# One run for each step of a merge, a decay mask by select, and a cast on ScalarE, in a hybrid DeltaNet and pooling block

## The chip, the cores and the metric

The kernel runs on one core of a Trainium2 chip. The metric is the device time of one execution in microseconds (us), the median of three runs. The engines are TensorE (PE in the rows, its weight loads PEld), VectorE (DVE), ScalarE (ACT), GpSimd (POOL), and SyncE (SP), which issues the DMAs.

## The reference

One layer over 1024 latent tokens of width 1024, with 256 context tokens ahead of them that use the same weights:

```
hn   = rms_norm(h, gain) * (1 + scale) + shift
proj = hn @ w_in                    # q, k, v | a, b | z_dn | u_pool | z_pool
q, k, v = split(silu(conv5(qkv)));  q, k = l2(q), l2(k)
o_f  = gated_delta_rule(q, k, v, g[0], beta[0], s_f)     # 8 heads of 128
o_b  = the same, backwards, from s_b                     # s_f, s_b: states after the context
o    = rms_norm(o_f + o_b, dn_gain) * silu(z_dn)
y_p  = (group-wise (box_mean(u_pool) - u_pool) @ pool_w) * pool_scale * silu(z_pool)
out  = rms_norm(x + gate * (concat(o, y_p) @ w_out), final_gain)

# gated_delta_rule, in chunks:
decay = exp(where(row >= col, g_row - g_col, -inf))
a     = where(row > col, (k*beta) @ k.T * decay, 0)
u, w  = solve(I + a, [v*beta, k*beta*exp(g)])
v_new = u - w @ S;   o = (q*exp(g)) @ S + (q @ k.T * decay) @ v_new
S     = S * exp(g_last) + (k*exp(g_last - g)).T @ v_new
```

## The kernel before

The products of the projections are fp32, made of three passes of a faster type: every operand is split into a high part, a copy in the type FP32R, and a low part, the difference, and high by high, low by high and high by low are summed. In the rows `hnhi, hnlo` are the parts of the normalised, transposed input, `wraw, whi, wlo` a weight tile and its parts (ScalarE makes `whi`, GpSimd `wlo`), and `mm` is the sum in PSUM. The input's own split stands in `x_half`, which transposes x by TensorE into `pp` and has ScalarE write the modulated input into `tmp`, `W`, `XT` or `Y`, and `x_split`, which copies that into `hnhi` and subtracts.

The delta rule works on chunks of 128 positions: 8 chunks of one head in both directions are one job, 8 heads and 2 context jobs make 10. For each job `stage_d` loads differences of summed decays into the tiles `D0` and `D1` (rows: `D`), masks them and takes the exponential. After a tile of k has been multiplied it is convolved on VectorE (`kT<-u,cw,kT`), goes through a tanh on ScalarE (`u<-kT`) and a last product (`kT<-u,kT`). Then `stage_a` multiplies k by itself (`pa<-kT`) and inverts the triangular matrices bottom up: blocks of 16 merge into blocks of 32 with products of 16 and 32 rows and columns (`pa<-laneN,B`, `pa<-laneN,bt`, `pa<-t,XT`), and `stage_b` merges 32 into 64 and 64 into 128 (`pp` from `W`, `B`, `Y`, `VV`). These are the small products: they use a corner of TensorE's array. A scan over the 8 chunks then carries the state (`sc<-S,kT`, `o<-S,qd`, `sc<-r,B`, `sc<-y,ks`, `o<-y,D`). A finished head is normalised (squares `junk<-o`, a power `sm<-sm,expo`, scaling `ks<-o,sm`), transposed (`pp<-ident,ks`) and multiplied by its gate (`zs<-pp,dng,zs`).

The order of each engine's instructions is fixed when the program is built. A planner (`Flow`) runs the generators of all these stages side by side: each `yield` is a place at which a thread may rest while another one issues, and a main thread supplies products of the projections in between. The planner keeps a modelled clock for each engine and charges every instruction with the price that `Engine.cost` returns; an instruction is put in when its inputs are ready by that clock. `yield REST` in `stage_a` and `stage_b` divides a step of a merge into groups of 16 or 8 small products, and the other work comes between. A helper records all operations, so every row of the profile has the same line, L364, and the rows are told apart by their tiles.

Of the kernel before, what the change touches and what calls it, by code (L numbers as in the profile page):

```python
# [27 lines left out]
TAKE = ("bank",)  # L28
RB = 8
REST = 340.0  # L30
NEXT = dict(pe=200.0, act=200.0, dve=200.0, pool=120.0)
# [282 lines left out]
class Engine:  # L314
    def __init__(self, flow, real, name):
        self.flow, self.real, self.name = flow, real, name

    def cost(self, op, a, k):
        out = k["out"] if "out" in k else a[0]
        n = _size(out)  # L320
        if self.name == "pe":
            if op == "transpose":
                return 108.0
            rhs = a[2] if len(a) > 2 else k["rhs"]
            n = _size(rhs)
            if rhs.dtype == FP32R:
                return max(107.0, 0.417 * n)
            m = int(out.shape[0])
            return max(1.67 * m, 1.67 * n) if m > 32 or n > 64 else max(0.83 * m, 0.83 * n)
        ptr = any(not isinstance(k.get(i), (float, int, type(None))) for i in ("scale", "bias", "scalar", "scalar1"))  # L330
# [12 lines left out]
        if op == "tensor_copy":  # L343
            return 80.0 + 3.8 * n
        if op == "memset":
            return 36.0 + 0.83 * n
# [44 lines left out]
def kernel(  # L391
# [90 lines left out]
    ident = const.tile([P, P], FP32, name="ident")  # L482
    mask = [const.tile([P, P], FP32, name=f"mask{d}") for d in range(2)]
    tri = [dl_tile([P, P], "S", 2) for d in range(2)]
# [48 lines left out]
    for d in range(2):  # L533
        pool.memset(mask[d], 0.0)
        pool.memset(tri[d], 1.0)
        s = 1 if d == 0 else -1
        pool.affine_select(out=mask[d], in_=mask[d], pattern=[[s, P]], compare_op=ALU.is_ge, fill=NEG,
                           base=0, channel_multiplier=-s)
        pool.affine_select(out=tri[d], in_=tri[d], pattern=[[s, P]], compare_op=ALU.is_ge, fill=0.0,
                           base=0, channel_multiplier=-s)  # L540
# [428 lines left out]
    def stage_d(J, part):  # L969


        t = J.PT[part] = dl_tile([P, 2, 4, P], f"D{part}", 2)
        r = J.h * (NB if J.is_x else NBC)
        for d in range(2):
            rd = r + 4 * (part ^ d)
            sync.dma_start(out=t[:, d].rearrange("p b i -> p (b i)"), in_=gscr[J.is_x][d, rd:rd + 4, :].rearrange(
                "b i -> (b i)").partition_broadcast(P))
        yield
        for d in range(2):
            pool.tensor_tensor(out=t[:, d], in0=t[:, d], in1=rep(mask[d], 4), op=ALU.add)  # L980
            if d or DY < 8:
                yield
            for b in range(4):
                act.activation(out=t[:, d, b, :], in_=t[:, d, b, :], func=ACTF.Exp,
                               bias=J.col("ngc", d, 4 * (part ^ d) + b))
                if b % DY == DY - 1:
                    yield "act" if XACT & 16 else None
        flow.flag("D", J.key, part)

    def stage_a(J):  # L990
# [103 lines left out]
        for d in range(2):  # L1094
            for b in range(8):
                for r in range(4):
                    w = tb[h16[r], b, :] if d else B[h16[r], 0, b, Q[r]]
                    pe.matmul(pv[Q[r], d, b, :], w, W16[h16[r], 8 * d + b, :], start=True, stop=True)
                if b % 4 == 3:
                    yield REST  # L1100
        yield
# [4 lines left out]
        for d in range(2):  # L1106
            for b in range(8):
                for r in range(4):
                    pe.matmul(pv2[Q[r], d, b, :], XT[Q[r], d, b, :], G[Q[r], d, b, :], start=True, stop=True)
                if b % 4 == 3:  # L1110
                    yield REST
        yield
# [17 lines left out]
    def stage_b(J):  # L1130
# [6 lines left out]
        for b in range(8):  # L1137
            for s in range(2):
                lo, hi = Q[2 * s], Q[2 * s + 1]
                pe.matmul(pv[hi, b, 0:32], B[lo, 0, b, hi], W[lo, 0, b, :], start=True, stop=True)  # L1140
                pe.matmul(pv[lo, b, 0:32], B[hi, 1, b, lo], WT[hi, b, :], start=True, stop=True)
            if b % 4 == 3:
                yield REST
        yield
# [5 lines left out]
        for b in range(8):  # L1150
            for s in range(2):
                lo, hi = Q[2 * s], Q[2 * s + 1]
                pe.matmul(pv[lo, b, 0:32], Y[hi, b, 0:32], B[hi, 0, b, hi], start=True, stop=True)
                pe.matmul(pv[hi, b, 0:32], Y[lo, b, 0:32], W[lo, 1, b, :], start=True, stop=True)
            if b % 4 == 3:
                yield REST
        yield TAKE
# [18 lines left out]
        for b in range(8):  # L1176
            pe.matmul(pv[h1, b, :], B[h0, 0, b, h1], VV[h0, b, :], start=True, stop=True)
            pe.matmul(pv[h0, b, :], B[h1, 1, b, h0], VV[h1, b, :], start=True, stop=True)
            if b % 4 == 3:
                yield REST  # L1180
        flow.flag("merged", J.key)
# [6 lines left out]
        for b in range(8):  # L1188
            pe.matmul(pv[h0, b, :], Y[h1, b, :], B[h1, 0, b, h1], start=True, stop=True)
            pe.matmul(pv[h1, b, :], Y[h0, b, :], B[h0, 1, b, h0], start=True, stop=True)  # L1190
            if b % 4 == 3:
                yield REST
        yield
# [194 lines left out]
    def x_half(hf):  # L1388
        for k in range(KT):
# [9 lines left out]
            if XACT & 4:  # L1399
# [3 lines left out]
                           scale=md[:, 0, 1, k:k + 1], bias=md[:, 0, 0, k:k + 1])  # L1403
            flow.give()
            flow.flag("h32", n)
            flow.add(x_split(hf, k, h32), [("h32", n)], True)

    def x_split(hf, k, h32):
        if XACT & 8:
            yield "dve"  # L1410
        dve.tensor_copy(hn[2 * hf][:, k, :], h32)
        yield
        e = dve if k % XD == 0 else pool
# [70 lines left out]
    def thread_a():  # L1484
# [3 lines left out]
        for k in range(-2, H):  # L1488
            yield ("k", k)
            yield ("ab", k >= 0)  # L1490
            yield ("done", k - 2)
            yield from stage_a(jobs[k])

# [589 lines left out]
```

## Time and profile before

| | |
|---|---|
| runs | 1317.15 us median, 1315.63 to 1318.1 |
| the profiled execution | 1321.76 us, span 1320.0 us |
| TensorE busy | 1212.5 us, 92% of the span |
| VectorE, ScalarE, GpSimd busy | 928.0, 570.8, 438.7 us |
| to 55 us | modulation of the inputs |
| 55 to 165 us | context, transposes and split of x |
| 165 to 1003 us | the eight heads |
| 1003 to 1146 us | pooling |
| 1146 to 1320 us | output projection |

A row of the timeline gives the start, the duration, engine, operation, tiles, the shape and how many alike stood together; in brackets the idle time ahead and what ended it. Matmuls overlap in the array, so what one costs is the distance between two starts (its pitch), not its duration. The rows count a small product or one of 128x128, which run in fp32, as two.

### The profile page before, as it was taken

The numbers are of one execution on the slowest core, as the hardware profiler recorded it, in microseconds if no ns is written. First come the engines' busy times: TensorE is split into PE (matmuls) and PEld (weight loads), VectorE is DVE, ScalarE is ACT, GpSimd is POOL, SyncE is SP. The second block draws the span as 40 slices with busy tenths as digits, with TensorE's granted clock in tenths as the row PEclk, the third lists the DMA queues.
The fourth block names the chain that finished last, engine by engine and source line by source line (L and its number), as shares of the span: only waits on it lengthen the run. The fifth ranks groups of instructions, "written<-read, shape, count | busy, mean of one in ns | idle before, by whom it ended". The sixth has DMA issues, their size and how long they took to land.

```text
span 1320.0 us, 26398 instructions
## 1 busy us (share of the span) xinstructions
PE 1212.5 (92%) x10631; PEld 977.8 (74%) x10631; DVE 928.0 (70%) x1883; ACT 570.8 (43%) x1498; POOL 438.7 (33%) x451
## 2 busy tenths in 40 slices
PE   8876699899899999999999989999999999799997
PEld 2666577677777877788778768778788777688887
DVE  4799989868886787877776867878433999724212
ACT  3466437444436547455474464643613123322110
POOL 2477433230421423314132233141215454402330
PEclk9788899899999999989999999999999899899999
DMA  9533344223121213212221131212313135565230
GB/s 329 188 99 93 86 140 125 74 57 90 37 49 48 78 42 100 58 46 80 49 83 44 41 100 41 69 63 43 103 60 109 48 104 185 199 206 157 83 112 32
DMA packets 157384, 123.73 MB, mean 94 GB/s; under 512 B 47106, under 2 KB 135115, under 8 KB 157261
## 3 DMA queue, kind: packets, MB, share of 16 engines
q1 hardware_dynamic: 157261, 122.04, 30.6%
q8 instruction: 83, 1.36, 0.4%
q14 instruction: 40, 0.33, 0.1%
HBM read 101.43 MB, written 20.60 MB: 92 GB/s over the span
## 4 chain that ended last, share of the span: by engine, by line
PE 40%; DVE 14%; ACT 6%; DMA 2%; issue 2%; POOL 2%; DVEq 0%; SPq 0%; POOLq 0%; ACTq 0%
PE mm L364 24%; PE sc L364 5%; PE o L364 4%; DVE kT L364 4%; PE pp L364 3%; PE pa L364 3%; DVE t L364 3%; DVE ws L364 3%; ACT junk L364 2%; ACT ks L364 1%; DMA D<-gscr 1%; DVE dlo L364 1%; DVE rp L364 1%; POOL wlo L364 1%; DVE zp L364 1%
## 5 line engine op out<-in xcount | busy, mean ns | idle before, releaser
L364 PE MATMUL mm<-hnhi,whi 128*128 128x512 f32 x768 | 321.0, 418 | 0.9 <-ACT whi L364 0.9
L364 PE MATMUL mm<-hnhi,wlo 128*128 128x512 f32 x768 | 316.7, 412 | 2.0 <-POOL wlo L364 2.0
L364 PE MATMUL mm<-hnlo,whi 128*128 128x512 f32 x768 | 316.9, 413 | 0.0
L364 POOL TENSOR_TENSOR wlo<-wraw,whi 128x512 fp32r<-128x512 f32 x110 | 158.0, 1442 | 337.3 <-ACT whi L364 330.5
L364 PEld LDWEIGHTS mm<-hnhi,whi 128*128 128x128 f32 x768 | 147.7, 192 | 26.8 <-issue 1.7
L364 PEld LDWEIGHTS mm<-hnhi,wlo 128*128 128x128 f32 x768 | 146.9, 191 | 26.0 <-POOL wlo L364 2.5
L364 PEld LDWEIGHTS mm<-hnlo,whi 128*128 128x128 f32 x768 | 147.6, 192 | 22.9
L364 DVE SCALAR_TENSOR_TENSOR kT<-u,cw,kT 128x512 f32<-128x512 f32 (+1 forms) x96 | 94.8, 994 | 5.3 <-ACT kT L364 1.8
L364 POOL TENSOR_TENSOR D<-D,mask 128x512 f32<-128x512 f32 x40 | 58.9, 1478 | 92.3 <-DMA D<-gscr 76.8
L364 ACT ACTIVATE y<-sc 128x256 f32<-128x256 f32 (+1 forms) x65 | 24.9, 383 | 131.3 <-PE sc L364 125.3
L364 ACT ACTIVATE u<-mm 128x512 f32<-128x512 f32 (+1 forms) x64 | 34.8, 543 | 88.3 <-PE mm L364 88.1
L364 DVE SCALAR_TENSOR_TENSOR t<-t,laneN 128x1 f32<-128x1 f32 (+4 forms) x150 | 68.0, 453 | 6.8 <-DMA laneN<-ds 2.8
L364 ACT ACTIVATE whi<-wraw 128x512 fp32r<-128x512 f32 x110 | 67.5, 633 | 1.8 <-DMA wraw<-in_w_in_dram 1.5
L364 DVE SCALAR_TENSOR_TENSOR vT<-u,cw,vT 128x512 f32<-128x512 f32 (+1 forms) x80 | 67.2, 843 | 1.5
L364 DVE TENSOR_TENSOR pw<-mm,zp 128x512 f32<-128x512 f32 (+1 forms) x12 | 8.0, 669 | 83.9 <-PE mm L364 83.9
L364 ACT ACTIVATE D<-D,ngc 128x128 f32<-128x128 f32 x160 | 53.1, 403 | 30.7 <-POOL D L364 30.7
L364 DVE SCALAR_TENSOR_TENSOR qT<-u,cw,qT 128x512 f32<-128x512 f32 (+1 forms) x80 | 63.0, 788 | 2.9 <-ACT qT L364 1.2
L364 DVE SCALAR_TENSOR_TENSOR S<-S,egl,sc 128x128 f32<-128x128 f32 x112 | 33.7, 343 | 33.4 <-PE sc L364 30.4
L364 DVE SCALAR_TENSOR_TENSOR r<-sc,neg,vn 128x128 f32<-128x128 f32 x128 | 38.7, 345 | 23.0 <-PE sc L364 22.9
L364 PEld LDWEIGHTS sc<-S,kT 128*128 128x128 f32 x256 | 36.9, 192 | 15.6 <-issue 9.1
L364 PE MATMUL mm<-D,whi 128*128 128x256 f32 x128 | 41.2, 322 | 7.3 <-DVE ks L364 4.5
L364 PE MATMUL sc<-S,kT 128*128 128x128 f32 x256 | 40.7, 282 | 7.2 <-DVE S L364 6.7
(409 smaller groups left out, 2785.5 us busy)
## 6 DMA issues: line engine op xcount, KB each, us to landing
wraw<-in_w_in_dram SPq DMA_DIRECT2D x55, 512.0 KB, 3.8
D<-gscr SPq DMA_DIRECT2D x40, 256.0 KB, 4.1
qd<-escr SPq DMA_DIRECT2D x16, 512.0 KB
kT<-in_w_in_dram SPq DMA_DIRECT2D x9, 512.0 KB, 4.0
whnhi<-in_w_mod_dram SPq DMA_DIRECT2D x8, 512.0 KB, 3.5
whnlo<-in_w_mod_dram SPq DMA_DIRECT2D x8, 512.0 KB, 9.5
D<-in_w_mod_dram SPq DMA_DIRECT2D x8, 512.0 KB, 4.9
yscr<-zs SPq DMA_DIRECT2D x8, 512.0 KB, 2.8
```

Of the source, the lines that this page charges most:

```text
L364: return f(*a, **k)
```

## The change

The small products of one step of a merge are issued without a pause. `Engine.cost` prices TensorE anew: 165 ns for each turn between whole-array and small products, and other prices for both. GpSimd masks the decays by a select along positions where it added a mask tile, and the two mask tiles go. ScalarE makes `hnhi` of x, where VectorE did. The first context job's `stage_a` waits for the first half of x (`("xt", 0)`).

```diff
-RB = 8
-REST = 340.0
+DRAIN = 165.0
@@ Engine.cost
             if op == "transpose":
-                return 108.0
+                turn = 0.0 if self.whole else DRAIN
+                self.whole = True
+                return turn + 108.0
...
-            if rhs.dtype == FP32R:
-                return max(107.0, 0.417 * n)
             m = int(out.shape[0])
-            return max(1.67 * m, 1.67 * n) if m > 32 or n > 64 else max(0.83 * m, 0.83 * n)
+            small = int(rhs.shape[0]) < P and m < P
+            turn = DRAIN if small == self.whole else 0.0
+            self.whole = not small
+            if small:
+                return turn + (60.0 if m > 32 else 17.0)
+            return turn + (max(120.0, 0.417 * n + 13.0) if rhs.dtype == FP32R else max(224.0, 1.67 * n + 13.0))
...
+        if op == "affine_select":
+            return 80.0 + 1.7 * n
@@ stage_d
-            pool.tensor_tensor(out=t[:, d], in0=t[:, d], in1=rep(mask[d], 4), op=ALU.add)
+            s = 1 - 2 * d
+            pool.affine_select(out=t[:, d], in_=t[:, d], pattern=[[0, 4], [s, P]], compare_op=ALU.is_ge, fill=NEG,
+                               base=0, channel_multiplier=-s)
@@ stage_a, twice; stage_b, four times
-                if b % 4 == 3:
-                    yield REST
@@ x_half
             flow.give()
+            act.activation(out=hn[2 * hf][:, k, :], in_=h32, func=ACTF.Copy)
             flow.flag("h32", n)
             flow.add(x_split(hf, k, h32), [("h32", n)], True)
+        flow.flag("xt", hf)
@@ x_split
-        dve.tensor_copy(hn[2 * hf][:, k, :], h32)
-        yield
@@ thread_a
             yield ("done", k - 2)
+            yield ("xt", 0)
             yield from stage_a(jobs[k])
```

Since the prices order everything, the order of all engines changes. Three places follow, each with the rows of before and then those of the change. A row is its position, its line, the operation, what it writes and reads, the shape and how many stand together; these lists count a product once, where the profile's rows count an fp32 one twice.

The first is TensorE in the merge of 16 into 32 of one job, before:

```order
1436 L364 MATMUL pa<-laneN,B 32x16 x16
1437 L364 MATMUL sc<-y,ks 128x128 x2
1438 L364 MATMUL pa<-laneN,B 32x16 x16
1439 L364 MATMUL o<-y,D_2349 128x128 x2
1440 L364 MATMUL pa<-laneN,bt 32x16 x16
1441 L364 MATMUL mm<-hnhi_235,whi 128x512
1442 L364 MATMUL mm<-hnlo_236,whi 128x512
1443 L364 MATMUL pa<-laneN,bt 32x16 x16
```

The same step of the same job with the change:

```order
1412 L371 MATMUL mm<-hnhi_225,wlo 128x512
1413 L371 MATMUL pa<-laneN,B 32x16 x32
1414 L371 MATMUL pa<-laneN,bt 32x16 x32
1415 L371 MATMUL sc<-y,ks 128x128 x2
1416 L371 MATMUL pp<-qT,kT 128x128 x4
1417 L371 MATMUL pa<-t_4276,XT 32x16 x64
```

Four groups of 16, with scan and projection between, became one of 64, and the second product of the step follows as another 64. Over the program 164 separate stretches of small products become 70: of those into `pa` 74 become 20, of the 32 by 32 ones into `pp` 50 become 30, of the 64 by 64 ones 40 become 20. The number of small products, 2400, stays.

The second place is VectorE around the convolution of the fourth head's k, which ends in `kT<-u,kT`, before:

```order
627 L364 SCALAR_TENSOR_TENSOR zs<-pp,dng,zs 128x512
628 L364 SCALAR_TENSOR_TENSOR vT<-u,vT 128x512 x2
629 L364 SCALAR_TENSOR_TENSOR zs<-pp,dng,zs 128x512
630 L364 SCALAR_TENSOR_TENSOR kT<-u,cw,kT 128x512 x2
631 L364 TENSOR_SCALAR VV<-pp 32x8x32 x2
632 L364 SCALAR_TENSOR_TENSOR kT<-u,cw,kT 128x512 x6
633 L364 SCALAR_TENSOR_TENSOR zs<-tmp,mm 128x512
634 L364 TENSOR_SCALAR B<-pp 64x8x64
635 L364 SCALAR_TENSOR_TENSOR kT<-u,kT 128x512 x2
```

With the change:

```order
606 L371 SCALAR_TENSOR_TENSOR zs<-pp,dng,zs 128x512
607 L371 TENSOR_SCALAR B<-pp 64x8x64
608 L371 SCALAR_TENSOR_TENSOR zs<-pp,dng,zs 128x512
609 L371 SCALAR_TENSOR_TENSOR kT<-u,cw,kT 128x512 x8
610 L371 SCALAR_TENSOR_TENSOR zs<-tmp,mm 128x512
611 L371 SCALAR_TENSOR_TENSOR kT<-u,kT 128x512 x2
```

All eight taps now follow the second `zs<-pp`, and the evacuations of the merge (`VV`, `B`) have moved ahead of them. On TensorE, between the second four transposes `pp<-ident,ks` that feed this `zs` and the `pa<-kT` that waits for the last row, there stood 45 projection products of 512 columns, 8 transposes and 5 stretches of small products; there now stand 44 such products and 4 transposes.

The third place is TensorE at the end of the last head's scan, before:

```order
3754 L364 MATMUL sc<-r,B 128x128 x2
3755 L364 MATMUL mm<-hnhi_233,wlo 128x512
3756 L364 MATMUL mm<-hnhi_233,whi 128x512
3757 L364 MATMUL mm<-hnlo_234,whi 128x512
3758 L364 MATMUL mm<-hnhi_233,wlo 128x512
3759 L364 MATMUL o<-y,D_9591 128x128 x2
...
3784 L364 MATMUL pp<-ident,ks 128x128 x8
```

With the change:

```order
3715 L371 MATMUL mm<-hnlo_226,whi 128x512
3716 L371 MATMUL mm<-hnhi_225,wlo 128x512
3717 L371 MATMUL sc<-r,B 128x128 x2
3718 L371 MATMUL o<-y,D_9742 128x128 x2
3719 L371 MATMUL pp<-ident,ks 128x128 x8
3720 L371 MATMUL mm<-hnhi_223,whi 128x512
```

The 24 projection products that stood between the scan's last product and the transposes, and the four between `sc<-r,B` and `o<-y,D`, have moved ahead of the scan's last step.

## Rows read from the trace of the kernel before

**Rows 1.** The page of the profile: busy time of each engine, its share of the span and the number of instructions; and the chain of work that ended last, by engine.

```profile
PE 1212.5 (92%) x10631; PEld 977.8 (74%) x10631; DVE 928.0 (70%) x1883; ACT 570.8 (43%) x1498; POOL 438.7 (33%) x451
PE 40%; DVE 14%; ACT 6%; DMA 2%; issue 2%; POOL 2%; DVEq 0%; SPq 0%; POOLq 0%; ACTq 0%
```

**Rows 2.** Busy time by stretch, the one from 55 to 165 us: stretch, its length, busy us and instructions of TensorE, its weight loads, VectorE, ScalarE and GpSimd, the granted TensorE clock, the DMA share and GB/s.

```profile
55.00:165.00 110.00, 74.33 (x459) 67.24 (x458) 106.51 (x187) 61.23 (x147) 71.96 (x87) 0.86 0.33 93
```

**Rows 3.** The timeline of TensorE where one merge's second product stands once as 16 small products and once as 48 (in the rows each counts double: x32, x96).

```profile
311.00 0.39 PE L364 MATMUL mm<-hnhi,whi 128*128 128x512 f32 x1
311.23 0.40 PE L364 MATMUL mm<-hnlo,whi 128*128 128x512 f32 x1
311.56 0.44 PE L364 MATMUL pa<-t,XT 32*32 32x16 f32 x32
311.93 0.50 PE L364 MATMUL mm<-hnhi,wlo 128*128 128x512 f32 x1
312.36 0.99 PE L364 MATMUL pa<-t,XT 32*32 32x16 f32 x96
313.28 1.16 PE L364 MATMUL pp<-qT,kT 128*128 128x128 f32 x8
```

**Rows 4.** VectorE's copies into `hnhi` between 55 and 165 us, grouped: busy us, mean ns of one, idle time ahead of them; and behind them the tile's own view for those from `W`: shortest, median and longest in ns.

```profile
L364 DVE CAST hnhi<-XT 128x512 fp32r<-128x512 f32 x4 | 6.2, 1554 | 0.0
L364 DVE CAST hnhi<-tmp 128x512 fp32r<-128x512 f32 x4 | 4.0, 1003 | 0.2 <-ACT tmp L364 0.2
L364 DVE CAST hnhi<-W 128x512 fp32r<-128x512 f32 x4 | 2.7, 683 | 0.0
L364 DVE CAST hnhi<-Y 128x512 fp32r<-128x512 f32 x4 | 2.6, 638 | 0.0
...
L364 DVE CAST hnhi<-W x4: 411/416/1490, 84.2 to 126.6; 128x512 fp32r<-128x512 f32 x4
```

**Rows 5.** The timeline of VectorE at one of these copies.

```profile
78.16 1.58 DVE L364 CAST hnhi<-tmp 128x512 fp32r<-128x512 f32 x1
79.66 1.50 DVE L364 SCALAR_TENSOR_TENSOR vT<-u,cw,vT 128x256 f32<-128x256 f32 x1
```

**Rows 6.** The timeline of GpSimd at the same time.

```profile
78.11 1.27 POOL L364 TENSOR_TENSOR D<-D,mask 128x512 f32<-128x512 f32 x1
79.41 2.90 POOL L364 TENSOR_TENSOR wlo<-kT,whi 128x512 fp32r<-128x512 f32 x2
```

**Rows 7.** Groups of GpSimd (the add of the mask, selects of 256 and of 128 columns) and of ScalarE (a copy of 512 columns): count, busy us, mean ns of one, idle time ahead.

```profile
L364 POOL TENSOR_TENSOR D<-D,mask 128x512 f32<-128x512 f32 x40 | 58.9, 1478 | 92.3 <-DMA D<-gscr 76.8 <-PE sc L364 10.2 <-DVE qd L364 5.3
L364 POOL TENSOR_SCALAR_AFFINE_SELECT t<-t 128x256 f32<-128x256 f32 x10 | 5.5, 545 | 0.7
L364 POOL TENSOR_SCALAR_AFFINE_SELECT S<-S 128x128 f32<-128x128 f32 x2 | 0.6, 292 | 0.0
...
L364 ACT ACTIVATE whi<-wraw 128x512 fp32r<-128x512 f32 x110 | 67.5, 633 | 1.8 <-DMA wraw<-in_w_in_dram 1.5
```

**Rows 8.** The timelines of TensorE, ScalarE and GpSimd at the end of the last head's scan, in order of time.

```profile
996.82 0.60 PE L364 MATMUL o<-y,D 128*128 128x128 f32 x4
...
1000.95 1.63 POOL L364 TENSOR_TENSOR sm<-sm,expo 128x8 f32<-128x8 f32 x1 [7.10 <-DVE sm L364]
...
1002.61 2.17 ACT L364 ACTIVATE ks<-o,sm 128x128 f32<-128x128 f32 x8 [1.95 <-POOL sm L364]
...
1003.03 2.13 PE L364 MATMUL pp<-ident,ks 128*128 128x128 f32 x8
```

**Rows 9.** What TensorE waited for between 165 and 1003 us, by tile: us in all, times, longest.

```profile
PE pa L364 <- DVE kT L364: 12.4, 7, 3.6
PE sc L364 <- ACT y L364: 9.2, 6, 2.1
PE sc L364 <- DVE S L364: 6.7, 5, 1.7
```

**Rows 10.** The timelines of TensorE, VectorE, ScalarE and GpSimd around the fourth head's k, in order of time.

```profile
507.53 0.60 PE L364 MATMUL pp<-ident,ks 128*128 128x128 f32 x4
...
509.10 2.61 DVE L364 SCALAR_TENSOR_TENSOR kT<-u,cw,kT 128x512 f32<-128x512 f32 x2
...
512.64 4.63 DVE L364 SCALAR_TENSOR_TENSOR kT<-u,cw,kT 128x512 f32<-128x512 f32 x6
...
518.65 4.75 POOL L364 TENSOR_TENSOR qd<-qd,qT 128x1024 f32<-128x1024 f32 x2
...
519.49 1.11 ACT L364 ACTIVATE u<-kT 128x1024 f32<-128x1024 f32 x1
...
521.78 3.84 DVE L364 SCALAR_TENSOR_TENSOR kT<-u,kT 128x512 f32<-128x512 f32 x2
...
524.00 1.16 PE L364 MATMUL pa<-kT 128*128 128x128 f32 x8 [0.26 <-DVE kT L364]
```

**Rows 11.** The timeline of TensorE behind a wait at the second head's `pa<-kT`.

```profile
344.91 1.41 PE L364 MATMUL pa<-kT 128*128 128x128 f32 x8 [3.62 <-DVE kT L364]
...
347.39 0.63 PE L364 MATMUL mm<-hnhi,whi 128*128 128x512 f32 x1
347.82 0.63 PE L364 MATMUL mm<-hnlo,whi 128*128 128x512 f32 x1
```

**Rows 12.** Busy time and granted clock of the stretch behind that wait, columns as in rows 2.

```profile
345.70:349.10 3.40, 3.40 (x12) 2.73 (x11) 1.85 (x3) 0.00 (x0) 0.00 (x0) 0.50 0.57 167
```

More of the change, by code (lines that the diff above doesn't have):

```diff
@@ L322, in cost @@
             if op == "transpose":
-                return 108.0
+                turn = 0.0 if self.whole else DRAIN
+                self.whole = True
+                return turn + 108.0
             rhs = a[2] if len(a) > 2 else k["rhs"]
             n = _size(rhs)
-            if rhs.dtype == FP32R:
-                return max(107.0, 0.417 * n)
             m = int(out.shape[0])
-            return max(1.67 * m, 1.67 * n) if m > 32 or n > 64 else max(0.83 * m, 0.83 * n)
+            small = int(rhs.shape[0]) < P and m < P
[4 more added lines that the diff above has]
+            return turn + (max(120.0, 0.417 * n + 13.0) if rhs.dtype == FP32R else max(224.0, 1.67 * n + 13.0))
         ptr = any(not isinstance(k.get(i), (float, int, type(None))) for i in ("scale", "bias", "scalar", "scalar1"))
@@ L482 @@
     ident = const.tile([P, P], FP32, name="ident")
-    mask = [const.tile([P, P], FP32, name=f"mask{d}") for d in range(2)]
     tri = [dl_tile([P, P], "S", 2) for d in range(2)]
@@ L533 @@
     for d in range(2):
-        pool.memset(mask[d], 0.0)
         pool.memset(tri[d], 1.0)
         s = 1 if d == 0 else -1
-        pool.affine_select(out=mask[d], in_=mask[d], pattern=[[s, P]], compare_op=ALU.is_ge, fill=NEG,
-                           base=0, channel_multiplier=-s)
         pool.affine_select(out=tri[d], in_=tri[d], pattern=[[s, P]], compare_op=ALU.is_ge, fill=0.0,
@@ L1109, in stage_a @@
                     pe.matmul(pv2[Q[r], d, b, :], XT[Q[r], d, b, :], G[Q[r], d, b, :], start=True, stop=True)
-                if b % 4 == 3:
-                    yield REST
         yield
@@ L1141, in stage_b @@
                 pe.matmul(pv[lo, b, 0:32], B[hi, 1, b, lo], WT[hi, b, :], start=True, stop=True)
-            if b % 4 == 3:
-                yield REST
         yield
@@ L1154, in stage_b @@
                 pe.matmul(pv[hi, b, 0:32], Y[lo, b, 0:32], W[lo, 1, b, :], start=True, stop=True)
-            if b % 4 == 3:
-                yield REST
         yield TAKE
@@ L1178, in stage_b @@
             pe.matmul(pv[h0, b, :], B[h1, 1, b, h0], VV[h1, b, :], start=True, stop=True)
-            if b % 4 == 3:
-                yield REST
         flow.flag("merged", J.key)
@@ L1190, in stage_b @@
             pe.matmul(pv[h1, b, :], Y[h0, b, :], B[h0, 1, b, h0], start=True, stop=True)
-            if b % 4 == 3:
-                yield REST
         yield
@@ L1404, in x_half @@
             flow.give()
+            act.activation(out=hn[2 * hf][:, k, :], in_=h32, func=ACTF.Copy)
             flow.flag("h32", n)
             flow.add(x_split(hf, k, h32), [("h32", n)], True)
+        flow.flag("xt", hf)
     def x_split(hf, k, h32):
-        if XACT & 8:
-            yield "dve"
-        dve.tensor_copy(hn[2 * hf][:, k, :], h32)
-        yield
+        yield "pool" if k % XD else "dve"
         e = dve if k % XD == 0 else pool
```

## The prediction, made before the changed kernel ran

> **What bounds the kernel now.** I read the page's busy shares and its chain first [rows 1]. TensorE is busy for 92% of the span, and it holds 40% of the chain against VectorE's 14%, ScalarE's 6% and GpSimd's 2%. So an order that takes work off TensorE shortens the kernel, where no wait follows that another engine ends. Then I read the stages. From 55 to 165 us the picture is another one: TensorE is busy for 74.33 of 110 us, at a granted clock of 0.86, and VectorE for 106.51 [rows 2]. There VectorE is the bound. In the heads TensorE's waits are few: 12.4 us for the finished k at `pa<-kT`, 9.2 us for ScalarE's `y` and 6.7 us for VectorE's `S` in the scan [rows 9].
>
> Last I looked at what a turn between whole-array and small products costs. Two projection products start 0.23 us apart; the first small product starts 0.33 us after the projection product ahead of it, 0.10 more. A stretch of 16 takes 0.37 us to the next start, one of 48 takes 0.92: 32 more cost 0.55, or 0.017 each, so that 16 should take 0.27 and a fixed 0.10 remains. The projection product after the 16 has 0.43 us to the next start, which holds its 0.23, the entry into the 48 and 0.10 more [rows 3]. A separate stretch thus costs 0.30 us beside its products.
>
> **The change, part by part.**
>
> *Fewer stretches.* 164 become 70, 94 fewer. I price those of 32 and 64 columns by the same 0.30, since their operands enter and leave the array in the same manner. 94 x 0.30 = 28 us less TensorE work, about 2.8 us in each of the 10 jobs.
>
> Not all of it reaches the end. The scan's waits for `y` and `S` [rows 9] are ended by engines whose work does not shrink, and what TensorE saves ahead of such a wait becomes a longer wait. There are 11 of them, about one or two in a head, and between two of them most of a head's merges lie open. I give back 5 us, with bounds of 0 (all these waits have slack behind other work) and 16 (as much again as they are now, 9.2 + 6.7).
>
> *The copies of x.* The 16 copies took VectorE 6.2 + 4.0 + 2.7 + 2.6 = 15.5 us; undisturbed ones take 0.416 [rows 4], 6.7 us together. The long ones ran beside GpSimd: 1.58 us at 78.16 over a GpSimd add that began at 78.11 [rows 5, 6]. The next VectorE instruction, a product of 128x256 that reads two tiles, took 1.50 us over the next GpSimd subtraction. So the lost time belongs to GpSimd's work and passes on to whatever VectorE does next; the sure gain is 6.7, the upper bound 15.5, the lower bound 0, if this stretch comes to hang on ScalarE or on the transposes. I take 6.5. On "SBUF — State Buffer", section "Who interferes with whom", the Trainium skill says the same: an instruction of VectorE in a two-port mode, or with two inputs in SBUF, and an instruction of GpSimd that reads SBUF exclude each other for the whole instruction, and ScalarE never waits. By that rule the gain would be the 6.7, since the remaining work of VectorE here mostly has two inputs, against 15.5 if only the copies were stretched; the trace agrees, with 1.50 us for the product behind the copy.
>
> ScalarE gets 16 copies of 0.633 us [rows 7], 10 us more on 61.23 of 110 [rows 2]. It has room, but its transposed inputs and these copies now stand in one queue. The new order also runs the 14 context tiles first and then the transposes with little between, which is why the lower bound is 0.
>
> *The mask.* GpSimd's add takes 1.48 us, 40 times. A select of 512 columns does not occur before; 128 columns take 0.292 and 256 take 0.545 [rows 7], 0.253 for 128 more, which gives an estimate of 1.05. GpSimd wins 9 us (against the shortest add in these rows, 1.27 [rows 6]) to 17 us, nearly all of it hidden: it is busy for a third of the span and holds 2% of the chain [rows 1]. What it hides behind is the wait for the load of the decays, 76.8 of the 92.3 us that the add's rows show ahead of it [rows 7]. I take 1 us, bounds 0 and 4. The mask of the same block as a select still reads SBUF, so VectorE is shut out for a little less time, and not never.
>
> *The end of the last scan.* Before, 24 projection products lie between the scan's last `o<-y,D` at 996.82 and the transposes at 1003.03; in that time ScalarE squares, GpSimd raises to a power (1.63 us at 1000.95) and ScalarE scales from 1002.61 [rows 8]. None of it waits for TensorE's products between. In the new order nothing is between. So TensorE will stand still for 6.2 us less the 0.4 of `o<-y,D` itself, 5.8, and some 0.4 more at `o<-y,D`, which has lost its four products ahead. The 24 products have been done earlier, but that time is already in the sum, since TensorE's work is the same. A wait of 3.62 us was followed by 3.4 us at a granted clock of 0.50, 1.2 GHz, where projection products start 0.43 us apart and not 0.23 [rows 11, 12]: eight products at 0.20 more, 1.6 us. Together 8 us, bounds 6 and 10 (two such stretches).
>
> *The cover of the k tiles.* In the third, fourth and fifth head the evacuations of the merge now stand ahead of the taps, and the stretches of small products ahead of the last transposes. For the fourth head, TensorE had 524.00 - 507.53 = 16.5 us from those transposes to `pa<-kT`, and waited 0.26 of it [rows 10]. In the new order 44 projection products and four transposes lie there: 44 x 0.23 and 0.6 for four transposes such as those at 507.53, 10.7 us, 5.8 less. What must happen in them: from 507.53 to the first tap at 509.10, 1.6; eight taps at 4.63/6 = 0.77, 6.2; the tanh, 1.1, and the last product's first half, some 0.7, which makes 9.6 us, if ScalarE takes the tanh at once (at 519.49 it came 2.2 us behind the taps' end at 517.27) and GpSimd's `qd` products do not lie on the last product again (3.84 us for two, at 521.78 [rows 10]). Without these two nothing waits; with both as before, 16.5 us are needed again and 5.8 are exposed, and 1.6 of slow clock behind it. I take a quarter, 1.4 us, in each of three heads: 4 us, bounds 0 and 3 x 7.4 = 22.
>
> **Sum.** -28 + 5 - 6.5 - 1 + 8 + 4 = -18.5 us. The profiled execution took 1321.76 us, 4.6 above the median of the runs; on it the change gives 1303, and on the median of 1317.15 it gives 1298.6. I forecast 1298.5 us. By the bounds that are likely together (5 more or less returned, the copies 3 to 13, the k tiles 0 to 12) this case lies between 1289 and 1307.
>
> **The rivals.**
>
> *The saving comes back as waits.* Every engine's order changes, and if the scan is held by the chain through ScalarE and VectorE in more places than the 11 of now, 16 us of the 28 return and not 5. Its price is 11 us: 1309.5, in a range of 1307 to 1315. For it: TensorE holds only 40% of the chain [rows 1]. Against it: its waits in the heads, the three rows together, are 28.3 us of 838 [rows 9]; the scan's instructions mostly find their inputs ready.
>
> *The stretch from 55 to 165 us gains all it can.* If the long copies go without handing their time on, it is 15.5 and not 6.5: 1289.5, and with all of the scan's 5 kept 1284.5. For it: VectorE is busy in 97% of that stretch [rows 2]. Against it: the 1.50 us of the next product [rows 5].
>
> *Slower, by the k tiles.* The mechanism of the fourth head holds wherever the planner has brought TensorE's rows nearer to the end of the convolution, and that may be in the sixth to eighth head too, six in all. If each pays 5.8 + 1.6 = 7.4 us, that is 44 us against the 22.5 that all other terms gain; if four of the six pay, 29.6 - 22.5 = 7.1 us slower, 1324.3. It decides from 22.5/6 = 3.75 us in each head. For it: the new prices give the taps of VectorE no more than before, and those stretch beside GpSimd, as 2.61 us for two taps at 509.10 against 4.63 for six at 512.64 shows [rows 10]. Against it: the evacuations that stood among the taps and the ScalarE work that delayed the tanh are out of the way.
>
> *The change does not do what it says.* The fixed cost could belong to every 16 small products and not to the stretch; then the 48 of rows 3 would have taken three times the 0.37 of the 16, 1.1 us, and the joined stretches would give nothing. They took 0.92, and the joining itself stands in the new order, so this has no chance of its own.
>
> **How the numbers follow.** My forecast's case has 0.62, the returned saving 0.16, the full gain from 55 to 165 us 0.08, the slower case 0.11, and 0.03 is left for what I do not see. Three hundredths of the second case and part of the last lie within 0.2% of 1317.15, 1314.5 to 1319.8, which is about what a measurement of this kernel can tell from no change. So: faster by more than that 0.82, within it 0.06, slower 0.12. The range from 1284 to 1316 holds the first three cases but for their edges.
>
> **What would show it.** On the profile of the changed kernel: small products into `pa` in rows of 64 and 128, and TensorE's busy time lower by some 28 us; 16 copies into `hnhi` on ScalarE near 0.63 us and the stretch to the first head's merges shorter by 3 to 13 us; the select near 1.05 us; a wait of 5 to 7 us at the last `pp<-ident,ks`, with a clock of 0.50 behind it; at `pa<-kT` of the third to fifth head waits between 0 and 3 us. The prediction is wrong if those last are near 6 us, if the scan's waits for `y` and `S` in the heads exceed 35 us together, or if the transposes of x leave TensorE idle longer than now.

## The result, and the profile after

The changed kernel takes 1332.82 us (median; 1331.48 to 1334.64), against 1317.27 for the kernel before in the same session: a ratio of 1.0121, 95% interval 1.0103 to 1.0138. It is 15.6 us slower, where 18.6 faster was forecast, and it lies outside the range.

The page after: busy time by engine, and the chain that ended last, as [rows 1].

```profile
PE 1206.5 (91%) x10631; PEld 981.7 (74%) x10631; DVE 901.6 (68%) x1867; ACT 580.7 (44%) x1514; POOL 411.6 (31%) x447
PE 49%; DVE 26%; ACT 11%; DMA 5%; issue 5%; POOL 2%; SPq 0%; DVEq 0%; POOLq 0%; ACTq 0%
```

TensorE is busy for 6.0 us less, not 28, and the chain holds more of every engine that TensorE waits for, with "issue" at 5% against 2%. That share is no measure of TensorE's own waits for "issue", which are shown below: select_and_copies, an experiment, has 4% of it and none of those waits. The span and the mean granted clock of the two, and then the stretch of the eight heads (columns as in [rows 2]), before first and after second in each pair:

```profile
core 0: 1320.0 us, clock 0.962
...
core 0: 1332.9 us, clock 0.951
```
```profile
165.00:1003.00 838.00, 795.28 (x8683) 647.71 (x8681) 621.09 (x1447) 415.93 (x1190) 240.48 (x234) 0.98 0.24 69
...
165.00:1003.00 838.00, 782.27 (x8670) 648.43 (x8669) 609.37 (x1445) 412.47 (x1172) 218.25 (x229) 0.96 0.25 69
```

In these 838 us TensorE stands idle for 838.00 - 782.27 = 55.7 us against 42.7, and runs at a lower clock; the last head now ends behind them. For the whole span I split the time in three: idle is span less busy; span x (1 - clock) is what the slower clock cost, an upper bound, since some of the slow time is idle; the rest is work at full clock. The mean clock has three decimals, so the last two columns are good to some 0.7 us.

| | span | idle | lost by clock | work |
|---|---|---|---|---|
| before | 1320.0 | 107.5 | 50.2 | 1162.3 |
| after | 1332.9 | 126.4 | 65.3 | 1141.2 |
| difference | +12.9 | +18.9 | +15.1 | -21.1 |

So the turns were saved: 21 us of work went. Idle time and a slower clock took 34. What TensorE waited for after, from 165 to 1015 us (us in all, times, longest), against [rows 9]:

```profile
PE pa L371 <- issue: 10.4, 9, 2.3
PE pa L371 <- DVE kT L371: 10.2, 4, 5.2
PE pp L371 <- ACT junk L371: 8.1, 7, 1.7
PE sc L371 <- DVE S L371: 7.1, 8, 2.0
PE sc L371 <- ACT y L371: 6.9, 4, 2.7
PE pp L371 <- ACT ks L371: 5.6, 1, 5.6
```

The waits for k and `y` are shorter than before; those for `junk`, ScalarE's squares, were 3.5 us before. New are `ks`, which was forecast, and "issue", in which TensorE waits for nothing that the profile shows. "Issue" stands at one place of the code, the second product of the 16 into 32 merge. The timeline of TensorE there, and the DMA queue of instructions in the same four microseconds (packets, MB, share of 16 engines):

```profile
485.37 0.69 PE L371 MATMUL pa<-laneN,B 16*32 16x16 f32 x62
...
485.93 0.70 PE L371 MATMUL pa<-laneN,bt 16*32 16x16 f32 x62
486.56 0.71 PE L371 MATMUL sc<-S,kT 128*128 128x128 f32 x4
487.10 1.06 PE L371 MATMUL pp<-qT,kT 128*128 128x128 f32 x8
488.09 0.82 PE L371 MATMUL pa<-t,XT 32*32 32x16 f32 x77
489.78 0.61 PE L371 MATMUL pa<-t,XT 32*32 32x16 f32 x51 [0.86 <-issue]
```
```profile
q8 instruction: 1, 0.02, 2.0%
```

The second run breaks off after 77 of its 128 rows. One instruction packet is under way meanwhile (2.0% of 16 engines x 4 us, 1.3 us; in the records it begins at 487.04), and TensorE goes on 1.4 us after its end.

### The profile page after: what moved, and what is told of

It reads as the page before. It is cut to its first block, busy times and chain, and to the rows that moved or that the text cites. A ratio compares the mean times of both kernels' runs of the same rounds, so it can differ in the third digit from the quotient of the medians.

```text
span 1332.9 us, 26418 instructions
## 1 busy us (share of the span) xinstructions
PE 1206.5 (91%) x10631; PEld 981.7 (74%) x10631; DVE 901.6 (68%) x1867; ACT 580.7 (44%) x1514; POOL 411.6 (31%) x447
## 3 DMA queue, kind: packets, MB, share of 16 engines
q8 instruction: 83, 1.36, 0.4%
## 4 chain that ended last, share of the span: by engine, by line
PE 49%; DVE 26%; ACT 11%; DMA 5%; issue 5%; POOL 2%; SPq 0%; DVEq 0%; POOLq 0%; ACTq 0%
PE mm L371 29%; DVE kT L371 6%; PE sc L371 6%; PE pp L371 5%; PE o L371 5%; DVE t L371 4%; PE pa L371 4%; DVE ws L371 3%; ACT junk L371 3%; DVE vT L371 3%; ACT ks L371 2%; DVE rp L371 1%; DVE qT L371 1%; DMA wraw<-yscr 1%; ACT u L371 1%
## 5 line engine op out<-in xcount | busy, mean ns | idle before, releaser
L371 PE MATMUL mm<-hnhi,wlo 128*128 128x512 f32 x768 | 321.4, 419 | 0.0
L371 PE MATMUL mm<-hnlo,whi 128*128 128x512 f32 x768 | 320.9, 418 | 0.0
L371 PEld LDWEIGHTS mm<-hnhi,whi 128*128 128x128 f32 x768 | 150.6, 196 | 26.4 <-issue 2.0
L371 PEld LDWEIGHTS mm<-hnlo,whi 128*128 128x128 f32 x768 | 150.3, 196 | 25.2
L371 PEld LDWEIGHTS mm<-hnhi,wlo 128*128 128x128 f32 x768 | 150.3, 196 | 24.7
L371 DVE SCALAR_TENSOR_TENSOR kT<-u,cw,kT 128x512 f32<-128x512 f32 (+1 forms) x96 | 90.4, 948 | 8.4 <-ACT u L371 3.9
L371 ACT ACTIVATE y<-sc 128x256 f32<-128x256 f32 (+1 forms) x65 | 24.9, 383 | 112.1 <-PE sc L371 84.5
L371 DVE SCALAR_TENSOR_TENSOR t<-t,laneN 128x1 f32<-128x1 f32 (+4 forms) x150 | 56.3, 375 | 22.1 <-DMA laneN<-ds 10.6
L371 ACT ACTIVATE u<-mm 128x512 f32<-128x512 f32 (+1 forms) x64 | 34.6, 541 | 77.7 <-PE mm L371 77.5
L371 ACT ACTIVATE D<-D,ngc 128x128 f32<-128x128 f32 x160 | 53.3, 413 | 30.6 <-POOL D L371 30.6
L371 PE MATMUL sc<-S,kT 128*128 128x128 f32 x256 | 42.7, 292 | 8.0 <-DVE S L371 7.1
L371 PE MATMUL mm<-D,wlo 128*128 128x256 f32 x128 | 39.8, 311 | 8.3 <-POOL wlo L371 8.3
L371 ACT ACTIVATE ks<-pp,sm 128x128 f32<-128x128 f32 x160 | 43.8, 401 | 8.0 <-PE pp L371 8.0
```

The source lines that it names most:

```text
L371: return f(*a, **k)
```

## The experiments

The changed kernel is three edits that act on each other: pauses out, new prices, and the select with the copies. Two questions were asked: is "issue" a lack of instructions, and which edit costs what. Every median is of 4 or 10 runs, since single runs of one kernel differ by up to 1%; profiles are single executions. All ratios are to the kernel before (1317.65 to 1318.43 us in these sessions). Idle time, loss by clock and work are reckoned as in the table above, from each run's own profile.

**Is TensorE short of instructions?** Two theories: the joined runs use up instructions faster than they are supplied; or a long run of small products itself brings the slow clock that is seen there.

*half_second.* The order of after, but the second product is issued as 32 products of 32 columns; the planner is charged for 64 (those lines are not shown). It leaves out every second block's own matrix.

```diff
-pe.matmul(pv2[Q[r], d, b, :], XT[Q[r], d, b, :], G[Q[r], d, b, :], ...)
+if b % 2 == 0: nc.tensor.matmul(pv2[Q[r], d, b:b + 2, :], XT[Q[r], d, b, :], G[Q[r], d, b:b + 2, :], ...)
```

> The changed kernel in its own order on every engine, but the second product of the 16-merge (pa<-t,XT) is issued as 32 products of 32 columns and not as 64 of 16, so its run has half the instructions; half of its values are wrong, and its matrix work is nearly the same. Theory 1 (instructions run out): the 10.4 us that TensorE waits for issue ahead of pa<-t,XT go to under 1 us, and most of the slow-clock stretches behind them go too, so the time falls by 15 to 30 us, to 1303 to 1318. Theory 2 (the long stretches of small products themselves bring the slow clock): the waits for issue go, but the stretches at 1.2 GHz behind these runs stay, 1320 to 1326. Theory 3 (only the new order of the engines costs): 1327 to 1333.

Measured: 1315.02 us, ratio 0.9973 (0.9949 to 0.9997), 17.8 below after. The "issue" waits fell from 10.4 to 4.0 us (2.2 at this product, 1.8 at `pp`), and the loss by clock from 65.3 to 57.8. It does not separate the theories, since the run is shorter too.

*half_first.* The same for the first product alone, with the same omission there; the second run, where the stalls are, stays whole.

```diff
-pe.matmul(pv[Q[r], d, b, :], w, W16[h16[r], 8 * d + b, :], ...)
+if b % 2 == 0: nc.tensor.matmul(pv[Q[r], d, b:b + 2, :], w, W16[h16[r], 8 * d + b:8 * d + b + 2, :], ...)
```

> The changed kernel in its own order, with the first product of the 16-merge (pa<-laneN) as 32 products of 32 columns and not 64 of 16, so that fewer instructions stand ahead of the second, which keeps its 64; half of the first one's values are wrong. Theory 1 (two refills of the instructions fall too near each other): the waits for issue at pa<-t,XT fall from 10.4 to under 5 us and with them the slow clock, 1313 to 1322. Theory 2 (the long run of the second product itself brings the slow clock): slow clock in the heads stays at 55 us or more, 1322 to 1328. Theory 3 (the second run alone is too long for the supply): waits stay near 10 us, 1326 to 1331.

Measured: 1315.18 us, 0.9983 (0.9965 to 1.0001), 17.6 below after. Its timeline at the same job, its clock, and its wait:

```profile
480.35 0.45 PE L1108 MATMUL pa<-laneN,B 16*32 16x32 f32 x32
...
482.56 1.26 PE L371 MATMUL pa<-t,XT 32*32 32x16 f32 x128
```
```profile
core 0: 1313.9 us, clock 0.958
```
```profile
PE pa L371 <- issue: 2.1, 3, 1.3
```

At this job the untouched second run now goes through in one piece; over all jobs 2.1 us of "issue" are left here and 2.4 at `pp`. The loss by clock falls from 65.3 to 55.2 us, work by 5.4, since instructions are gone, and idle by 3.5. So a run of 64 is not slow by itself. What precedes it, the number of instructions issued just before, makes it stall. That is the supply theory. That the 10 us of clock belong to the stalls is likely and not shown: whole_price_old (below) has more "issue" than after, 12.7 us, and a loss by clock of 55.1.

*gap_between.* After, with a longer rest ahead of the second product, so that 12 to 18 other matmuls stand between the two runs.

```diff
+yield 2000.0
 pv2 = ps[:, 256:512]...
```

> The changed kernel with the planner told to rest 2 us ahead of the second product, so that 12 to 18 other matmuls stand between the two runs of 64 where 3 to 9 stood; the runs stay whole. Theory 1: waits for issue under 3 us, less slow clock, 1312 to 1325 where the rest of the order stays as good. Theory 2: the runs are as long as before, slow clock 55 us or more in the heads, 1328 to 1336.

Measured: 1322.86 us, 1.0042 (1.0018 to 1.0066). Timeline, and the waits:

```profile
485.92 0.48 PE L371 MATMUL mm<-hnhi,wlo 128*128 128x512 f32 x1
486.33 1.26 PE L371 MATMUL pa<-t,XT 32*32 32x16 f32 x128
487.52 0.71 PE L371 MATMUL sc<-r,B 128*128 128x128 f32 x4
```
```profile
PE pa L371 <- DVE kT L371: 18.7, 7, 5.0
PE sc L371 <- ACT y L371: 16.1, 6, 3.0
```

No "issue" wait is left; nine of the ten second runs take 1.19 us to the next start, the tenth 1.37; in after they took 1.5 to 3.7. But the merge now ends later, and the waits for k and `y` rise to 34.8 us, from 17.1. So that the 10.0 us won are near the 10.4 of the "issue" waits is chance: by the profiles idle falls by 4.4 us, the loss by clock by 4.5 and work by 3.1.

*rest_second.* After, with a pause put back in the second product alone: groups of 16 again.

```diff
 pe.matmul(pv2[Q[r], d, b, :], XT[Q[r], d, b, :], G[Q[r], d, b, :], ...)
+                if b % 4 == 3:
+                    yield 340.0
```

> The changed kernel with the pause put back in the second product of the 16-merge alone (four runs of 16 for one of 64), the planner's other rules as changed. Theory 1 (instructions run out): waits for issue under 2 us; 30 more stretches cost 9 us; 1312 to 1325. Theory 2 (long stretches bring the slow clock): also better, by the clock and not by the waits. Theory 3 (new order): 1330 to 1342, the 9 us of turns on top.

Measured: 1341.47 us, 1.0166 (1.0137 to 1.0195): slower than after although "issue" fell. Its waits:

```profile
PE sc L371 <- ACT y L371: 15.1, 6, 2.9
PE pa L371 <- issue: 2.7, 4, 1.0
```

The stall is real but not the whole loss. Against after the loss by clock falls by 9.1 us, but work rises by 10.3, about what 30 more stretches at 0.30 us cost, and idle by 3.6: `y` alone, 6.9 us in after, now has 15.1.

**Which edit costs what?**

*before_no_pause.* The kernel before with the pauses out, nothing else.

```diff
-if b % 4 == 3:
-    yield REST
```
(six times)

> The kernel before with the pauses taken out of all merges and nothing else; old prices, old mask, old copies. Theory 1 (instructions run out): waits for issue ahead of pa<-t,XT of 8 to 14 us and slow clock behind them; the 22 us of fewer turns are given back; 1308 to 1325. Theory 3 (the new prices and their order cost): without them the saving shows, 1290 to 1300.

Measured: 1335.68 us, 1.0119 (1.0089 to 1.015): taking the pauses out costs 18 us by itself.

```profile
PE sc L364 <- DVE S L364: 14.3, 10, 2.6
PE pa L364 <- issue: 7.4, 8, 1.2
```

Work falls by 25.9 us (1162.3 to 1136.4), idle rises by 30.9 and the loss by clock by 9.9.

*after_old_prices.* After, with the prices of before for TensorE.

> The changed kernel with the old prices of TensorE in the planner; no pauses, select and copies on ScalarE as changed. Theory 1 (instructions run out): waits for issue of 8 to 14 us remain; 1318 to 1333. Theory 3 (new prices): most of the loss goes, 1300 to 1312.

Measured: 1315.86 us, 0.9971 (0.9948 to 0.9993). Its span, clock and busy time:

```profile
core 0: 1310.9 us, clock 0.958
...
PE 1192.5 (91%) x10631; PEld 979.2 (75%) x10631; DVE 901.8 (69%) x1867; ACT 581.0 (44%) x1514; POOL 407.9 (31%) x447
```

The prices cost 17 us on top of the other edits.

*only_prices.* Before, with the new prices alone.

> The kernel before with the new prices of TensorE alone, pauses, add and copies as before. Theory: within 8 us of the kernel before, 1310 to 1326. Rival (the new prices are at fault): 1325 to 1340.

Measured: 1366.93 us, 1.0375 (1.0356 to 1.0394), 49 us slower.

```profile
PE pa L371 <- DVE kT L371: 17.9, 6, 5.1
PE sc L371 <- ACT y L371: 16.2, 6, 3.3
```

*all_pauses.* After, with all pauses back.

> The changed kernel with the pauses put back in all six merges: new prices, select and copies on ScalarE stay. Theory (the joined stretches lose more by the supply of instructions, the slow clock and the bare end of the scan than the turns give): no waits for issue, cover at the end of the scan, 1305 to 1322. Rival (the new prices are at fault): 1325 to 1340.

Measured: 1363.82 us, 1.0365 (1.0333 to 1.0397). At the new prices taking the pauses out gains 31 us, at the old ones it loses 17 to 18. The edits don't add up.

*turn_price_0* and *whole_price_old.* After, with one price of TensorE changed: no charge for a turn; and the old charge for a product of 512 columns (213.5 ns in place of 226.5) and for those of 128.

```diff
-DRAIN = 165.0
+DRAIN = 0.0
@@ and, in the other kernel
-max(120.0, 0.417 * n + 13.0) if rhs.dtype == FP32R else max(224.0, 1.67 * n + 13.0)
+max(107.0, 0.417 * n) if rhs.dtype == FP32R else 1.67 * max(n, m)
```

> The changed kernel with the planner's price of a turn at 0 in place of 165 ns, all other prices new. If the turn's price is what brings the dependents too near: 1312 to 1322, near the 1315.9 of the kernel with all old prices. If the projection product's price is: 1328 to 1337, as the changed kernel.

> The changed kernel with the old price of whole-array products (213.5 ns for 512 columns in place of 226.5), the turn at 165 ns and the small products at 17 and 60 ns as changed. If the projection product's price is what brings the dependents too near: 1310 to 1322. If the turn's price is: 1328 to 1337.

Measured: 1351.9 us, 1.0249 (1.0208 to 1.0291), and 1314.76 us, 0.9973 (0.9958 to 0.9987). The charge for the turn helps by 19 us; 13 ns more on a whole product costs 18, all that the prices cost. From the second to after, idle goes from 118.9 to 126.4 us and the loss by clock from 55.1 to 65.3. Meanwhile "issue" falls, from 12.7 to 10.4, so the stalls are not what the dearer product costs. The waits for k, `y`, `S` and `ks` rise, from 14.1 to 29.8 us together. The traces show what precedes them: from `sc<-r,B` to the next `sc<-y,ks` stand on average 3.4 to 3.6 products of 512 columns in every kernel with the dearer product, and 3.7 to 4.5 in every one with the old price. The planner thus puts fewer between; that this is the whole cost no run tested.

*only_select* and *only_copies.* Before, with one of these edits (the second with its `("xt", 0)`, and with GpSimd in place of VectorE named at the rest of every second split).

> The kernel before with the mask by select alone. By the prediction's step: 1 us faster, at most 4; the select takes 1.05 us. Rival: its other duration in the planner moves the order and so the time by some us either way, 1308 to 1326.

> The kernel before with the 16 copies of x on ScalarE and the first context job waiting for the first half of x, nothing else. By the prediction's step: 6.5 us faster (0 to 13), the stretch to the first merges shorter by it. Rival: the new order gathers the transposes of x where nothing covers them, and the stretch to the first merge shortens by under 2 us; 1314 to 1319.

Measured: 1305.72 us, 0.9898 (0.9871 to 0.9925), and 1322.09 us, 1.0028 (1.001 to 1.0047). The select gains 12 us; the copies alone cost 4. The page of only_select:

```profile
PE 1212.6 (92%) x10631; PEld 976.1 (74%) x10631; DVE 914.9 (70%) x1883; ACT 572.1 (44%) x1498; POOL 414.7 (32%) x447
```

VectorE's 1883 instructions, as many as before, take 13.1 us less [rows 1].

*select_and_copies.* Both, with the pauses and prices of before.

> The kernel before with the select and with the copies on ScalarE, pauses and old prices kept. If the two add up (-12 and +4): 1306 to 1314. The kernel with old prices and no pauses has 1315.9: below 1312 here, taking out the pauses lost time also in that company; above 1320, it gained.

Measured: 1298.81 us, 0.984 (0.98 to 0.9881), the fastest, 34 us below after and 19 below before. Its span, clock and busy time, and TensorE's waits from 165 to 1003 us:

```profile
core 0: 1299.0 us, clock 0.970
...
PE 1201.3 (92%) x10631; PEld 966.1 (74%) x10631; DVE 904.9 (70%) x1867; ACT 582.6 (45%) x1514; POOL 414.3 (32%) x447
```
```profile
PE sc L364 <- DVE r L364: 9.3, 9, 1.7
PE sc L364 <- DVE S L364: 8.7, 9, 1.7
...
PE pa L364 <- DVE kT L364: 3.6, 1, 3.6
PE sc L364 <- ACT y L364: 0.8, 1, 0.8
```

Its work is that of before (1162.3); idle is 9.8 us less and the loss by clock 11.2. The waits for k and `y` went from 21.6 us [rows 9] to 4.4, and 8.6 came back at `r` and 2.0 at `S`.

**Is there a version with joined runs that gains?** *old_prices_gap* is after_old_prices with the rest of gap_between; *select_no_pause_gap* is before with the select, no pauses and that rest; *select_join_b* is before with the select and the pauses out of `stage_b` alone.

> The changed kernel with the old prices of TensorE and a rest of 2 us ahead of the second product of the 16-merge, so that 6 to 18 other matmuls stand between the two runs of 64. Theory 1 (two refills too near each other): the 9 us of waits for issue that the kernel with the old prices had go, 1300 to 1312. Rival (other waits take their place): 1313 to 1322.

> The kernel before with the select, without pauses in both merges, and with a rest of 2 us ahead of the second product of the 16-merge; old prices, copies on VectorE. If the supply of instructions was the main loss of the joined stretches: 1296 to 1306, as fast as the kernel with joined stretches in stage_b alone (1304.1) or faster. If other waits take the gain: 1307 to 1318.

> The kernel before with the mask by select and with the pauses taken out of stage_b alone; stage_a keeps its pauses, so no two long runs of 16-merges stand near each other. 40 stretches fewer, 12 us less turning; 10 and not 24 projection products cover the end of the last scan. Theory 1: no waits for issue, 3 us bare at the end, and against the kernel with the select alone 0 to 9 us faster, 1297 to 1306. Rival (every saved turn comes back as a wait): 1306 to 1316.

Measured: 1305.31 us, 0.9904 (0.9883 to 0.9924); 1306.83, 0.9919 (0.9896 to 0.9943); 1304.08, 0.9893 (0.9874 to 0.9911). With the old prices the gap gains 10.6 us, as with the new. Of old_prices_gap:

```profile
core 0: 1301.0 us, clock 0.966
...
PE 1183.6 (91%) x10631; PEld 968.8 (74%) x10631; DVE 898.0 (69%) x1867; ACT 580.2 (45%) x1514; POOL 404.9 (31%) x447
...
PE pa L366 <- issue: 1.3, 2, 0.8
```

Against after_old_prices "issue" falls by 7.8 us, yet idle falls by 1.0 alone, since waits for other engines take its place (k: 9.0 us for 4.9); the loss by clock falls by 10.9. But joining gains nothing beside the select: both kernels with the select alone of the other edits stand with only_select's 1305.72, and old_prices_gap stays 6.5 behind select_and_copies.

## Why the prediction was wrong

One way through the edits, by medians: before 1317.6; with select and copies 1298.8 (-19); with the pauses out as well 1315.9 (+17); with the new prices 1332.8 (+17). By another order the shares would differ, as all_pauses shows.

*Fewer stretches, -28 and +5 given back: the step that failed.* The work was sized well: at this step, from select_and_copies to after_old_prices, it falls by 24.9 us (1162.3 to 1137.4). The price of 0.30, read at products of 16 columns, holds for the wider ones too: in before all three sizes of stretch, where they stand between projection products, have 0.10 us ahead of them and 0.11 behind (medians). The failure is "I give back 5": idle rises by 20.7 us and the loss by clock, for which the term had nothing, by 16.1. (By the profiles the step costs 11.9 us, by the medians 17; beside the pauses it holds 5 ns in the planner's price of the select. before_no_pause, with the pauses alone, agrees: work 25.9 less, idle 30.9 and clock 9.9 more.) The waits for `y` and `S`, on which the bound of 16 rested, are not the reason; after they are 14.0 us together, where 35 was named as the sign of error. Of the idle time 9.1 us are the "issue" waits and 5.6 the wait for `ks` at the end of the scan, which the +8 below had foreseen; both stand in this view of after_old_prices (TensorE's waits, the whole span) and neither in that of select_and_copies:

```profile
PE pa L366 <- issue: 9.1, 9, 1.5
...
PE pp L366 <- ACT ks L366: 5.6, 1, 5.6
```

The remaining 6 us are spread over many waits. The prediction took TensorE's saved time as time by which it reaches the next engine's result sooner. It did not ask whether TensorE itself can be fed, and the pauses, which the prediction read as turns only, had spread the instructions. Spreading them again, by the gap, brought back 10.6 of the 17 us, nearly all by the clock. How much of the slow clock each stall or wait brings stays open.

*Prices.* The prediction let them act only by the order at three places, and gave them no term. They cost 17 us here, and 49 on the kernel before.

*The copies of x, -6.5.* Each copy takes ScalarE 0.63 us as forecast:

```profile
L371 ACT ACTIVATE hnhi<-tmp 128x512 fp32r<-128x512 f32 x4 | 2.5, 632 | 0.1
```

VectorE is relieved in the stretch (against [rows 2]):

```profile
55.00:165.00 110.00, 76.77 (x457) 68.53 (x458) 90.41 (x169) 69.99 (x160) 62.41 (x85) 0.83 0.32 90
```

It is 16.1 us less, near the bound of 15.5, but the select has a part in it: with the copies alone, over the whole span, VectorE's busy time falls by 9.3 us (928.0 to 918.7 in only_copies), between the sure 6.7 and the bound. So some of the lost time was handed on, as the prediction and the rule it cites have it. But TensorE's transposes then wait for ScalarE: for `W` 8.7 us in three waits, and from 55 to 165 us for its four tiles together 12.5 us, against 9.9 before. The prediction had named such a rise as a sign of error. The first merge begins only 1.5 us earlier (170.35 against 171.86), and in only_copies 1.2 later. The lower bound, "comes to hang on ScalarE or on the transposes", is what happened; alone the edit lost 4 us. Beside the select it gained 7 (1305.72 to 1298.81), near the 6.5, but not by this mechanism: the first merge then begins 3.2 us later (170.49 for 167.28). Why it gains there is open.

*The mask, -1: far too small.* The select takes less than the estimate of 1.05 us (in before, the add took 1.48 [rows 7]):

```profile
L371 POOL TENSOR_SCALAR_AFFINE_SELECT D<-D 128x512 f32<-128x512 f32 x40 | 31.2, 784 | 50.2 <-DMA D<-gscr 49.3 <-DVE qd L371 0.8
```

and it gained 12 us alone, 19 with the copies. "Nearly all of it hidden" followed GpSimd's own share of the chain; the gain shows in TensorE's waits for VectorE and ScalarE. Shown are those waits, and VectorE's 13.1 us less for as many instructions in only_select. That the shorter GpSimd instruction holds VectorE off for less time fits them; no run tests it apart from the order. The taps of the k tiles don't show it: 77.5 us in the heads of select_and_copies, 74.4 before. So part may be a luckier order.

*The end of the last scan, +8: right.* The wait is 5.57 us (5.8 forecast), the one at `o<-y,D` 0.52 (0.4):

```profile
1002.75 0.60 PE L371 MATMUL sc<-r,B 128*128 128x128 f32 x4
1003.88 0.71 PE L371 MATMUL o<-y,D 128*128 128x128 f32 x4 [0.52 <-ACT y L371]
1010.16 2.28 PE L371 MATMUL pp<-ident,ks 128*128 128x128 f32 x8 [5.57 <-ACT ks L371]
```

Half clock stands from 1007.1 to 1013.9, 6.8 us, of which 3.1 lie under the wait. TensorE is busy in 3.7 of them, which cost at most half of that, 1.9: with the two waits 8.0 us at most.

*The k tiles, +4: right in these heads.* The third to fifth head's `pa<-kT`:

```profile
441.45 1.16 PE L371 MATMUL pa<-kT 128*128 128x128 f32 x8 [2.13 <-DVE kT L371]
...
526.32 1.16 PE L371 MATMUL pa<-kT 128*128 128x128 f32 x8 [1.17 <-DVE kT L371]
...
612.70 1.16 PE L371 MATMUL pa<-kT 128*128 128x128 f32 x8 [1.72 <-DVE kT L371]
```

That is 4.2 us more than before in the three. At the second head the wait grew too, from 3.62 to 5.18; in the sixth to eighth, where it had been 2.7 us each, it vanished, and all together fell from 12.4 to 10.2. For the kernel the term had the wrong sign. So the rival that ended slower, by the k tiles, has the sign and not the mechanism. "The saving comes back as waits" is nearest, but its 11 us sat in the scan's `y` and `S`, which did not grow.

## What to carry to other kernels

Before instructions are packed closer, count them: a run of tiny products uses up the instruction supply many times faster than large ones (here 256 instructions in 2.2 to 3.4 us ahead of a stall, where the span's mean is 16), and interleaving that looks like a cost of turns may be what keeps the supply ahead. Where a planner's prices set the order, price the prices: change them alone, and each edit alone and joined, since here one edit lost 17 us or gained 31 by which prices stood beside it. A shorter instruction on an engine that seems hidden can pay through the engines that it holds up; look at what the bound engine waits for, not at the hidden engine's share of the chain.

## What the runs showed of the hardware

*Instructions come in blocks of 256, and TensorE can outrun them.* The nine "issue" stalls stand whole multiples of 256 instructions of TensorE apart, matmuls and weight loads counted and to within one: six times 1792 = 7 x 256, once 1536 and once 3327. The page's row for the queue:

```profile
q8 instruction: 83, 1.36, 0.4%
```

83 packets of 1.36 MB / 83 = 16 KB, and 2 x 10631 instructions / 256 = 83.05: a packet for each block. Two runs of 64 products are 256 instructions each, loads and matmuls (an fp32 product counting two); the 256 instructions up to a stall had lasted only 2.2 to 3.4 us, and TensorE resumed 1.3 to 1.5 us after the end of the packet. The Trainium skill, "Runtime: NRT & Kernel Launch", section "Instruction fetch mechanics", states that an engine's instruction memory is refilled in 16 KiB blocks of 256 instructions over a DMA queue of its own, and that the cost of crossing a block's end is mostly hidden. The trace agrees with the block; here the cost is not all hidden, at 10.4 us in nine waits.

*Slow clock beside such a stall.* The stretch behind the first one, columns as in [rows 2]:

```profile
174.30:181.10 6.80, 6.73 (x91) 5.08 (x92) 3.84 (x7) 4.69 (x11) 0.90 (x1) 0.50 0.27 77
```

6.8 us at the lower of the two levels, 1.2 GHz, in which TensorE is busy for 6.73. Six of the nine stalls of after have such a stretch, which overlaps the stall or begins within 1.1 us of its end; the six last 30.6 us, so by the table's measure 15.3 were lost in them. In whole_price_old it is seven of nine and 27.2 us (one begins 2.1 us behind), at a loss by clock in all of 55.1 against 65.3. So stalls and slow clock stand together, and the stalls alone do not decide how much is lost.
